# Offsets of matmul operands in SBUF: the low part of x's first quarter, one sum, and the first pair's kept weights

## The chip, the cores and the metric

The kernel runs on one core of a Trainium2 chip. The metric is the device time of one execution in microseconds; of the kernel before, three runs are at hand, and one further execution was profiled. Engines are named as in the profile: PE is TensorE (PEld its weight loads), DVE VectorE, ACT ScalarE, POOL GpSimd, SP SyncE.

## The reference

One decoder layer on x of 512 tokens by 1024 features, float32: a half-step SwiGLU FFN, a token mixer of two recurrent head groups, and a second half-step FFN, each between two RMS norms.

```python
x = x + 0.5 * rms_norm(swiglu_ffn(rms_norm(x, norm_pre[l, 0]), ffn1_w_in[l], ffn1_w_out[l]), norm_post[l, 0])
mixed = token_mixer(rms_norm(x, norm_pre[l, 1]), w_mix_in[l], ...)
x = x + rms_norm(mixed, norm_post[l, 1])
x = x + 0.5 * rms_norm(swiglu_ffn(rms_norm(x, norm_pre[l, 2]), ffn2_w_in[l], ffn2_w_out[l]), norm_post[l, 2])

def swiglu_ffn(x, w_in, w_out):
    gate, up = jnp.split(x @ w_in, 2, axis=-1)
    return (jax.nn.silu(gate) * up) @ w_out
```

The change touches the first product of the FFNs, x @ w_in, with 1024 rows and 2 x 2816 columns of weights.

## The kernel before

**Numbers in two parts.** A float32 value is held as a high part rounded to the matmul's format (fp32r) and a low part that is the rest. A product is three matmuls: high by high, high by low and low by high. ScalarE writes the high part of weights (L237), VectorE the low one (L239), out of a raw tile that a DMA filled.

**The FFN's first product.** The 22 column blocks of 128 are taken in 11 pairs (PAIRS). For a pair, x transposed is cut in four quarters by feature half and token half, the weights in four blocks a to d, and a scheme of seven products, p1 to p7, takes the place of the usual eight (products of sums of quarters). `prod` (L524) does one: 24 matmuls at L537, three parts by two column blocks of 128 by four k, each with 128x128 stationary weights and 128x256 moving values. The moving operand is `left[p]`: for p1 the quarter `xq[0]`, for p2 `xq[1]`; later p4 and p5 use `xq[3]` and `xq[2]`; p3, p6 and p7 use sums of quarters that lie in the three `s` tiles, `sq[0]`, `sq[2]`, `sq[1]`. For most products the parts come in the order high by high, high weights by the low moving part, low weights by the high moving part; c1 has the low moving part last.

Pair 0 is done by the usual eight products, because sums of quarters aren't there yet: c1 to c4 on the first token half (`xq[0]`, `xq[1]`), then e1 to e4 on the second with the same weights. Three of these weights (of c1, c3 and c4) are kept for e1, e3 and e4 in the `s` tiles, in the places `stay[1]`, `stay[2]`, `stay[0]`, before the sums overwrite them; c2's are in the ring of weights `w`. The order is written out by hand in `HEADS` and `ORDER` (L42 to L49): c1, c3, c2, c4, p1 of pair 1, e1, e3, e2, p1 of pair 2, p2 of pair 1, e4, p2 of pair 2, then p7, p5, p3, p6 of pair 1, p5, p7, p3, p4 (of pair 1), p6 of pair 2, then from pair 3 on p1, p4 of the pair before, p3, p5, p7, p6, p2 (in pair 3 a little different). In the first FFN `start` (L629) issues the head (c1 to p2 of pair 2), in the second `ffn_head` (L594). Transposes of x (L312) stand in the head: in the first FFN ahead of c4 and ahead of p1 of pair 1, in the second ahead of c3 and ahead of c4. In the first FFN one small transpose of parameters (L1020) stands ahead of p7 of pair 1.

**The second product** is at L794 and L802 in `ffn_out` (L765): there the weights move, and hidden values (`hs`, in the `s` tiles and in the tiles of x) are stationary. The mixer's projections read the same four tiles `xq` with the ordinary layout, through `xop` (L147).

**Places in SBUF.** `xq[n]` are four tiles of 2 x 1024 floats per partition (8192 bytes): high part, then low part, each four k of 256 tokens. The ring of weights is one tile `w` with room for four weights of 2 x 1024 floats, which `lie` (L202) places at PAD + 2048 n + d floats, with d of `LIES`. The `s` tiles have 2 x 1024 + PAD floats; sums lie in them from LATE = 112 floats on, except that the low part of the sum of p7 lies at 0 instead of at LATE + 1024: counted mod 512 bytes (128 floats) that is 64 bytes further. The kept weights lie at 0, except that the low part of the one of c1 lies at 1024 + NEAR (48 floats).

The head and the steady part of the first product are TensorE work in a fixed order; weights wait for a place in the ring (four in all, dropped after their product), and sums for the products that use what they overwrite.

The functions that the change touches, and those that call them:

Of the kernel before, what the change touches and what calls it, by code (L numbers as in the profile page):

```python
# [9 lines left out]
F32R = mybir.dt.float32r  # L10
# [4 lines left out]
P = 128  # L15
T = 512
D = 1024
# [2 lines left out]
ND = D // P  # L20
NF = FF // P
EPS = 1e-6
RAW, WBUF, PAD, LATE, NEAR, NEXT = 3, 4, 128, 112, 48, 64
PAIRS = NF // 2
HALF = T // 2
KH = ND // 2
# [40 lines left out]
class Load:  # L67


    def __init__(self, key, src, a, b, ring="raw", depth=3, ahead=3, group=None):  # L70
        self.key, self.src, self.a, self.b, self.ring, self.depth, self.ahead = key, src, a, b, ring, depth, ahead
        self.group = group
# [12 lines left out]
class Layer:  # L85
    def __init__(self, ctx, tc, aps):
        self.tc, self.nc = tc, tc.nc
        self.__dict__.update(aps)
        nc = self.nc
        pool = lambda name, **kw: ctx.enter_context(tc.tile_pool(name=name, bufs=1, **kw))  # L90
        self.cp, self.wp, self.sp, self.psp = pool("cp"), pool("wp"), pool("sp"), pool("psp", space=PSUM)
        self.uid, self.hold = 0, ()
        self.wt, self.free, self.slot = None, deque(), {}

        self.ident = self.cp.tile([P, P], F32, name="ident")
        make_identity(nc, self.ident)
        self.nhalf = self.cp.tile([P, 8], F32, name="nhalf")
        nc.gpsimd.memset(self.nhalf, -0.5)
        self.xs = self.cp.tile([P, NT, D], F32, name="xs")

        self.xq = [self.cp.tile([P, 2, KH, HALF], F32R, name=f"xq{n}") for n in range(4)]
        self.prm = self.cp.tile([P, 36], F32, name="prm")

    def nm(self, s):
# [42 lines left out]
    def xop(self, k, part, t0, t1):  # L147
        q = self.xq[2 * (t0 // HALF) + k // KH]
        return q[:, part, k % KH, t0 % HALF : (t1 - 1) % HALF + 1]
# [52 lines left out]
    def lie(self, kind):  # L202

        used = [o for _, o, _ in self.slot.values()]
        at = LIES[kind]

        first = 1 + (kind == "out")
        tries = [(n, d) for n in self.free for d in (at[:first] if n < 2 else at[first - 1 :: -1])]
        for n, d in tries + [(n, d) for d in at[first:] for n in self.free]:
            o = PAD + 2 * D * n + d  # L210
            if o + 2 * D <= self.wt.shape[1] and all(abs(o - a) >= 2 * D for a in used):
                return n, o

    def split(self):

        nc = self.nc
        it = self.items.popleft()
        raw = self.raw[it.key]
        _, a, b = raw.shape
        if it.dst:  # L220
            w = it.dst()
        else:
            if self.wt is None:
                self.wt = self.wp.tile([P, 2 * D * WBUF + 2 * PAD], F32R, name="w")
            if not self.slot and it.key[0] != "mix":
                self.free = deque(FREE)
            n, o = self.lie("out" if it.key[1] == "out" else "mix" if it.key[0] == "mix" and b == 512 else "any")
            self.free.remove(n)
            w = self.wt[:, o : o + 2 * D].rearrange("p (b k t) -> p b k t", b=2, k=a)
            self.slot[id(w)] = n, o, w  # L230
        hi, lo = self.both(w)
        if it.sums:
            raw, hi, lo = (self.flat(v)[:, QUARTER:] for v in (raw, hi, lo))
        self.ready.append((w, it.dst is not None))
        rows = it.rows
        if rows is None:
            nc.scalar.copy(hi, raw)  # L237
            yield
            nc.vector.tensor_tensor(lo, raw, hi.bitcast(F32), op=ALU.subtract)  # L239
        else:  # L240
            for j in range(a):
                nc.scalar.activation(hi[:, j], raw[:, j], AF.Copy, scale=rows[:, j : j + 1])
            yield
            for j in range(a):
                nc.vector.scalar_tensor_tensor(
                    lo[:, j], raw[:, j], rows[:, j : j + 1], hi[:, j].bitcast(F32), op0=ALU.mult, op1=ALU.subtract
                )
        with self.behind(*self.hold):
            for out, other in it.adds:
                o, c = self.raw[out], self.raw[other]  # L250

                late = out[1] >= HEAD
                (nc.vector if late else nc.gpsimd).tensor_tensor(o, o, c, op=ALU.add)  # L253
        if it.sums:
            self.sum_quarters(self.quarters(self.raw[it.key]))
        self.load_due(self.done)
        self.done += 1
        yield
# [14 lines left out]

        return w if isinstance(w, tuple) else (w[:, 0], w[:, 1])

    def place(self, t, a, late=False):

        o = LATE if late else 0
        return t[:, o : o + 2 * D].rearrange("p (b k t) -> p b k t", b=2, k=a)

    def feed(self, most=WBUF):

# [43 lines left out]
    def part(self, i, h, src):  # L326

        pv = self.turn(src, h)
        v = slice(i * P, (i + 1) * P)
        dst = self.xq[h][:, :, :, v]  # L330
        yield
        self.nc.scalar.copy(dst[:, 0], pv)
        yield
        self.nc.vector.tensor_tensor(dst[:, 1], pv, dst[:, 0].bitcast(F32), op=ALU.subtract)
        yield
        self.nc.scalar.copy(self.xf[h][:, :, v], pv)
        yield
# [167 lines left out]
    def open_ffn(self, ctx):  # L505

        hp = self.hpool = ctx.enter_context(self.tc.tile_pool(name=self.nm("hp"), bufs=1))
        self.hf = hp.tile([P, NF, T], F32, name=self.nm("hf"))
        self.xf = [self.hf[:, j : j + 2, :].rearrange("p a (b t) -> p (a b) t", t=HALF) for j in (NF - 4, NF - 2)]
        sq = [hp.tile([P, 2 * D + PAD], F32R, tag="s", bufs=3, name=self.nm("sq")) for _ in range(3)]  # L510
        self.sq = [self.place(t, KH, True) for t in sq]

        part = lambda o: sq[1][:, o : o + D].rearrange("p (k t) -> p k t", k=KH)
        self.sq = [self.both(self.sq[0]), (part(D + LATE), part(0)), self.both(self.sq[2])]
        xq = [self.both(x) for x in self.xq]
        self.stay = [self.place(t, KH) for t in sq]
        self.stay[1] = (self.stay[1][:, 0], sq[1][:, D + NEAR : 2 * D + NEAR].rearrange("p (k t) -> p k t", k=KH))
        self.left = {"p1": xq[0], "p2": xq[1], "p4": xq[3], "p5": xq[2], "p6": self.sq[2], "p7": self.sq[1], "p3": self.sq[0]}
        self.left.update({"c1": xq[0], "c2": xq[1], "c3": xq[0], "c4": xq[1]})
        self.left.update({"e1": xq[2], "e2": xq[3], "e3": xq[2], "e4": xq[3]})  # L520
        self.gs, self.held, self.copies = [], {}, []
        self.hs, self.bank, self.later, self.u, self.q, self.had = deque(), {}, deque(), {}, {}, set()
# [106 lines left out]
    def start(self, norm, xn):  # L629
# [8 lines left out]
        split = self.split()  # L638
        step(q[1][0], q[1][1])
        next(split)  # L640
        step(q[1][0])
        next(split)
        step(q[0][0], q[1][0])
        head = deque(HEADS)
# [74 lines left out]
    def x_place(self, *n):  # L719

        out = []
        for m in range(2):
            t = self.xq[n[m % len(n)]].rearrange("p b k t -> p (b k t)")
            o = PAD - LATE + NEXT + (D * m if len(n) == 1 else 0)
            out.append(t[:, o : min(o + D, 2 * D)])
        return out
# [949 lines left out]
```

## Time and profile before

| | us |
|---|---|
| three runs | 950.09, 950.67, 952.49 |
| median | 950.67 |
| profiled execution | 950.96 |
| its span, first to last instruction | 949.2 |
| PE busy | 938.8 |
| DVE busy | 774.5 |
| ACT busy | 489.4 |
| POOL busy | 119.4 |

The costliest groups of instructions on TensorE (busy us, mean ns of one, then idle time ahead of it):

```profile
L537 PE MATMUL ps<-xq,w 128*128 128x256 f32 x2016 | 237.9, 277 | 0.0
L537 PE MATMUL ps<-sq,w 128*128 128x256 f32 x1440 | 171.0, 277 | 0.0
L794 PE MATMUL ps<-w,hs 128*128 128x256 f32 x1344 | 158.9, 277 | 0.6 <-DVE ps L770 0.6
...
L482 PE MATMUL ps<-xq,w 128*128 128x256 f32 x480 | 56.4, 278 | 0.0
L802 PE MATMUL ps<-w,hs 128*128 128x256 f32 x336 | 40.3, 276 | 0.0
```

The page's group L537 `ps<-xq,sq` (288 matmuls in all) has the products of kept weights. Matmuls are pipelined: one is told with 276 ns or more from start to end, while the next starts some 113 to 118 ns later. So the pace is read from the differences between starts, not from the mean ns. In the order of time, matmuls of one line and the same tiles that follow each other without a gap stand as one row, with their count; the start of the next row less the start of this one is the time of the row. Offsets in a tile aren't in the profile; they come from the program.

### The profile page before, as it was taken

The page shows a single profiled execution, that of the slowest core. Times are in us where ns is not written, and L with a number is a line of the kernel's source. Part 1 is how long each engine was busy: PE and PEld are TensorE (multiplying, and loading weights), DVE is VectorE, ACT ScalarE, POOL GpSimd, SP SyncE. Part 2 cuts the span into 40 slices and gives each one's busy share as a digit, 9 for nine tenths or more (in the row PEclk, how much of TensorE's full clock was granted, in tenths as well). Part 3 has the DMA queues.
Part 4 walks back from the last instruction along what each step waited for, and adds up shares of the span by engine and source line. Part 5 has one row for each costly group of instructions (what it writes and reads, how often), then busy time and mean ns, then how long its engine had stood idle before and what let it go on. Part 6 is the DMA issues. An engine that isn't in the chain of part 4 may idle for free.

```text
span 949.2 us, 18146 instructions
## 1 busy us (share of the span) xinstructions
PE 938.8 (99%) x7531; PEld 905.0 (95%) x7531; DVE 774.5 (82%) x1052; ACT 489.4 (52%) x691; POOL 119.4 (13%) x176
## 2 busy tenths in 40 slices
PE   9999999999999999999999999999999999999997
PEld 7999999999999999998887888899999999999997
DVE  6899999999789776698846665797998899988983
ACT  7645444456446456956632444664444444654641
POOL 2530000000001045200011310354000000000101
PEclk9999999999999999999999999999999999999999
DMA  9244343344232024321212124324333333124202
GB/s 319 82 133 134 106 129 108 104 121 125 91 111 88 23 84 119 112 67 46 89 45 67 46 89 148 98 66 134 112 111 121 108 108 111 67 90 134 78 35 89
DMA packets 81677, 96.13 MB, mean 101 GB/s; under 512 B 4117, under 2 KB 61497, under 8 KB 81594
## 3 DMA queue, kind: packets, MB, share of 16 engines
q1 hardware_dynamic: 81306, 94.44, 31.4%
q8 instruction: 59, 0.97, 0.4%
q10 hardware_dynamic: 288, 0.52, 0.2%
q14 instruction: 24, 0.20, 0.1%
HBM read 92.85 MB, written 2.10 MB: 100 GB/s over the span
## 4 chain that ended last, share of the span: by engine, by line
PE 62%; DVE 1%; issue 0%; ACT 0%; POOL 0%; POOLq 0%; DVEq 0%; ACTq 0%
PE ps L537 23%; PE ps L794 8%; PE ps L482 6%; PE ps L143 5%; PE ps L145 5%; PE ps L144 5%; PE ps L802 3%; PE ps L1177 2%; PE ps L492 1%; PE ps L312 1%; PE ps L1351 0%; PE ps L1262 0%; PE ps L1458 0%; PE ps L1431 0%; PE ps L1217 0%; DVE w L239 0%
## 5 line engine op out<-in xcount | busy, mean ns | idle before, releaser
L237 ACT CAST w<-raw 128x1024 fp32r<-128x1024 f32 (+1 forms) x228 | 235.7, 1040 | 252.2 <-PE ps L537 92.0
L239 DVE TENSOR_TENSOR w<-raw,w 128x1024 fp32r<-128x1024 f32 (+1 forms) x228 | 281.8, 1242 | 42.0 <-ACT w L237 41.9
L537 PE MATMUL ps<-xq,w 128*128 128x256 f32 x2016 | 237.9, 277 | 0.0
L537 PEld LDWEIGHTS ps<-xq,w 128*128 128x128 f32 x2016 | 233.3, 188 | 0.0
L537 PE MATMUL ps<-sq,w 128*128 128x256 f32 x1440 | 171.0, 277 | 0.0
L537 PEld LDWEIGHTS ps<-sq,w 128*128 128x128 f32 x1440 | 167.4, 188 | 0.0
L794 PE MATMUL ps<-w,hs 128*128 128x256 f32 x1344 | 158.9, 277 | 0.6 <-DVE ps L770 0.6
L794 PEld LDWEIGHTS ps<-w,hs 128*128 128x128 f32 x1344 | 155.6, 188 | 0.9 <-issue 0.9
L253 DVE TENSOR_TENSOR raw<-raw,raw 128x1024 f32<-128x1024 f32 x64 | 80.1, 1252 | 0.6
L143 PE MATMUL ps<-w,xq 128*128 128x512 f32 x192 | 78.9, 411 | 0.1
L145 PE MATMUL ps<-w,xq 128*128 128x512 f32 x192 | 74.9, 392 | 0.0
L144 PE MATMUL ps<-w,xq 128*128 128x512 f32 x192 | 74.9, 391 | 0.0
L400 POOL TENSOR_SCALAR col<-col 128x1 f32<-128x1 f32 x24 | 10.1, 421 | 496.5 <-ACT junk L399 496.5
L482 PE MATMUL ps<-xq,w 128*128 128x256 f32 x480 | 56.4, 278 | 0.0
L482 PEld LDWEIGHTS ps<-xq,w 128*128 128x128 f32 x480 | 55.2, 188 | 0.5 <-issue 0.5
L253 POOL TENSOR_TENSOR raw<-raw,raw 128x1024 f32<-128x1024 f32 x16 | 43.1, 2695 | 51.2 <-DVE w L239 40.8
L143 PEld LDWEIGHTS ps<-w,xq 128*128 128x128 f32 x192 | 36.1, 188 | 8.3 <-issue 0.9
L145 PEld LDWEIGHTS ps<-w,xq 128*128 128x128 f32 x192 | 36.0, 188 | 8.1 <-DVE xq L319 0.3
L144 PEld LDWEIGHTS ps<-w,xq 128*128 128x128 f32 x192 | 36.2, 188 | 6.7 <-issue 0.2
L729 ACT CAST hs<-hf 128x1024 fp32r<-128x1024 f32 x28 | 29.4, 1050 | 22.2 <-PE ps L802 22.2
L802 PE MATMUL ps<-w,hs 128*128 128x256 f32 x336 | 40.3, 276 | 0.0
L802 PEld LDWEIGHTS ps<-w,hs 128*128 128x128 f32 x336 | 39.1, 188 | 0.0
(250 smaller groups left out, 1144.7 us busy)
## 6 DMA issues: line engine op xcount, KB each, us to landing
raw<-in_ffn_w_in_dram SPq DMA_DIRECT2D x88, 512.0 KB, 3.7
raw<-in_ffn_w_out_dram SPq DMA_DIRECT2D x44, 512.0 KB, 3.7
raw<-in_w_mix_in_dram SPq DMA_DIRECT2D x28, 512.0 KB, 3.7
raw<-in_w_mix_out_dram SPq DMA_DIRECT2D x8, 512.0 KB, 3.7
out_dram<-xs SPq DMA_DIRECT2D x8, 256.0 KB, 2.1
xs<-in_x_dram SPq DMA_DIRECT2D x6, 256.0 KB, 6.8
gpost<-in_norm_post_dram SPq DMA_DIRECT2D x3, 512.0 KB
gpre<-in_norm_pre_dram SPq DMA_DIRECT2D x2, 512.0 KB, 4.1
```

What stands on the lines that cost most here:

```text
L143: mm(ps, sh, mh, start=start, stop=False, **kw)
L144: mm(ps, sh, ml, start=False, stop=False, **kw)
L145: mm(ps, sl, mh, start=False, stop=stop, **kw)
L237: nc.scalar.copy(hi, raw)
L239: nc.vector.tensor_tensor(lo, raw, hi.bitcast(F32), op=ALU.subtract)
L253: (nc.vector if late else nc.gpsimd).tensor_tensor(o, o, c, op=ALU.add)
L482: mm(ps[:, u0:u1], w[:, a, k, :], self.xop(k, b, u0, u1), start=k + n + m == 0, stop=k == ND - 1 and n == 2, skip_group_check=True,)
L537: self.nc.tensor.matmul(ps[:, c], wb[b][:, k, v], left[d][:, k, :], start=first and a + n + k == 0, stop=n == 2 and k == KH - 1, skip_grou ...
L729: self.nc.scalar.copy(hi, src)
L794: mm(out, a[kk][:, i * P : (i + 1) * P], w[:, b, kk, QUARTER * v : QUARTER * (v + 1)], start=begin and c == kk == n == 0, stop=kk == 1 and ...
L802: mm(ps[:, QUARTER * c : QUARTER * (c + 1)], A[a][:, c], B[b], start=begin and c == n == 0, stop=n == 2, skip_group_check=True,)
L1177: nc.tensor.matmul(sc[:, 64 * m : 64 * m + 64], k8[:, m], q8[:, m], start=True, stop=True)
```

## The change

It moves operands; no instruction comes in or goes out.

- `xq[0]` becomes 2 x (1024 + 16) floats. In the view `xh[0]`, which `part` writes and which the products p1, c1 and c3 read, the low part lies 1024 + 16 floats behind the high one, so 64 bytes further mod 512 than before. The mixer and `x_place` keep the ordinary view of the same tile. The four tiles are allocated in the order 1, 2, 3, 0, the longer one last.
- The low part of the sum of p7 lies behind its high part like those of the other sums, at LATE + 1024.
- The kept weights lie at NEXT = 64 floats (256 bytes) in the `s` tiles, high and low part one behind the other, all three alike; NEAR is gone.
- The ring of weights begins at FRONT = 96 floats in its tile in place of PAD = 128, and the tile is 32 floats shorter; `xq[0]` is 32 floats longer.

```diff
-RAW, WBUF, PAD, LATE, NEAR, NEXT = 3, 4, 128, 112, 48, 64
+RAW, WBUF, PAD, LATE, NEXT, FRONT, STEP = 3, 4, 128, 112, 64, 96, 16
...
-        self.xq = [self.cp.tile([P, 2, KH, HALF], F32R, name=f"xq{n}") for n in range(4)]
+        xq = {n: self.cp.tile([P, 2 * D + 2 * STEP * (n == 0)], F32R, name=f"xq{n}") for n in (1, 2, 3, 0)}
+        self.xt = [xq[n] for n in range(4)]
+        self.xq = [t[:, : 2 * D].rearrange("p (b k t) -> p b k t", b=2, k=KH) for t in self.xt]
+
+        x0 = self.xt[0].rearrange("p (b x) -> p b x", b=2)[:, :, :D].rearrange("p b (k t) -> p b k t", k=KH)
+        self.xh = [x0, *self.xq[1:]]
...
-            o = PAD + 2 * D * n + d
+            o = FRONT + 2 * D * n + d
...
-                self.wt = self.wp.tile([P, 2 * D * WBUF + 2 * PAD], F32R, name="w")
+                self.wt = self.wp.tile([P, 2 * D * WBUF + FRONT + PAD], F32R, name="w")
...
-    def place(self, t, a, late=False):
-
-        o = LATE if late else 0
-        return t[:, o : o + 2 * D].rearrange("p (b k t) -> p b k t", b=2, k=a)
+    def place(self, t, o):
+
+        return t[:, o : o + 2 * D].rearrange("p (b k t) -> p b k t", b=2, k=KH)
...
-        dst = self.xq[h][:, :, :, v]
+        dst = self.xh[h][:, :, :, v]
...
-        self.sq = [self.place(t, KH, True) for t in sq]
-
-        part = lambda o: sq[1][:, o : o + D].rearrange("p (k t) -> p k t", k=KH)
-        self.sq = [self.both(self.sq[0]), (part(D + LATE), part(0)), self.both(self.sq[2])]
-        xq = [self.both(x) for x in self.xq]
-        self.stay = [self.place(t, KH) for t in sq]
-        self.stay[1] = (self.stay[1][:, 0], sq[1][:, D + NEAR : 2 * D + NEAR].rearrange("p (k t) -> p k t", k=KH))
+        self.sq = [self.both(self.place(t, LATE)) for t in sq]
+        xq = [self.both(x) for x in self.xh]
+        self.stay = [self.place(t, NEXT) for t in sq]
...
-            t = self.xq[n[m % len(n)]].rearrange("p b k t -> p (b k t)")
+            t = self.xt[n[m % len(n)]]
```

## The prediction

> **What bounds the kernel.** I read the page first, then the order of time of the matmuls, then the clock and the waits.
>
> ```profile
> PE 938.8 (99%) x7531; PEld 905.0 (95%) x7531; DVE 774.5 (82%) x1052; ACT 489.4 (52%) x691; POOL 119.4 (13%) x176
> ...
> PE ps L537 23%; PE ps L794 8%; PE ps L482 6%; PE ps L143 5%; PE ps L145 5%; PE ps L144 5%; PE ps L802 3%; PE ps L1177 2%; PE ps L492 1%; PE ps L312 1%; PE ps L1351 0%; PE ps L1262 0%; PE ps L1458 0%; PE ps L1431 0%; PE ps L1217 0%; DVE w L239 0%
> ```
>
> TensorE is busy 99% of 949.2 us and the chain of waits is made of its matmuls. No instruction is added or taken out, so only the pace of matmuls can change the time. That pace is read from the starts in the order of time (start us, us, then instruction and count); a row's 128x256 matmuls follow each other without a gap.
>
> ```profile
> 33.41 8.64 PE L537 MATMUL ps<-xq,w 128*128 128x256 f32 x72
> 41.90 2.99 PE L537 MATMUL ps<-xq,sq 128*128 128x256 f32 x24
> 44.72 2.99 PE L537 MATMUL ps<-xq,w 128*128 128x256 f32 x24
> 47.64 0.25 PE L1020 MATMUL ps<-ident,rows 36*128 36x36 f32 x1
> 47.82 3.10 PE L537 MATMUL ps<-sq,w 128*128 128x256 f32 x24
> 50.76 2.88 PE L537 MATMUL ps<-xq,w 128*128 128x256 f32 x24
> 53.48 5.60 PE L537 MATMUL ps<-sq,w 128*128 128x256 f32 x48
> 58.92 2.88 PE L537 MATMUL ps<-xq,w 128*128 128x256 f32 x24
> ```
>
> From 33.41 to 41.90, 72 matmuls take 8.49 us, 117.9 ns each. From 53.48 to 58.92, 48 of the same shape take 5.44 us, 113.3 ns each. So there are **two paces**: a product of 24 takes 2.83 us at the slow one and 2.72 us at the quick one, 0.11 us apart. The granted clock is 1.00 in both stretches (windows 24 to 47 and 53 to 81 us), so it is not the clock. The turn lies inside the product from 47.82 to 50.76: p7 of pair 1, the first product whose low moving part lies 64 bytes further. The second FFN does the same:
>
> ```profile
> 640.81 2.99 PE L537 MATMUL ps<-xq,sq 128*128 128x256 f32 x24
> 643.63 2.99 PE L537 MATMUL ps<-xq,w 128*128 128x256 f32 x24
> 646.46 3.00 PE L537 MATMUL ps<-sq,w 128*128 128x256 f32 x24
> 649.30 2.88 PE L537 MATMUL ps<-xq,w 128*128 128x256 f32 x24
> 652.02 5.60 PE L537 MATMUL ps<-sq,w 128*128 128x256 f32 x48
> ```
>
> 2.82 and 2.83 us, then p7 of pair 1 with 2.84, then 2.72. Two different products stand before it and one thing is common: the step of p7. I read it so: **the step of 64 bytes releases the slow pace**, for 0.01 us more than a slow product. In the quick pace the step has a price: p7 and its neighbour take 5.49 us, a pair without it 5.44 (53.48 to 58.92), so 0.05 us:
>
> ```profile
> 83.45 5.66 PE L537 MATMUL ps<-sq,w 128*128 128x256 f32 x48
> 88.94 8.32 PE L537 MATMUL ps<-xq,w 128*128 128x256 f32 x72
> ```
>
> **Places.** By the program's memory layout, counted mod 512 bytes, the quarters of x begin at 160, the places of weights in these products at 480, the three s tiles at 224. Nearly all stationary operands of the FFNs lie 320 bytes ahead of the moving one. Kept weights lie 64 ahead (224 - 160), the low part of the first pair's 256, p7's low part has its weights 256 ahead (480 - 224). After the change the kept weights lie at 320, p7 at 320, and p1, c1 and c3 meet their low moving part at 256: the geometry of p7, mod 512. The w tile begins 128 bytes later (xq0 is that much longer) and its places 128 earlier in it: they stay. Only small tiles behind xq and the raw ring move, by 128 bytes; VectorE and ScalarE read them, and no row shows a duration that hangs on this. Taken as nothing, covered by the lead that weights have over TensorE (below); slower reads would have to use up that lead before the end moved.
>
> **The sum, first FFN**, differences between starts, after minus before.
> - c1: enters slow, and exchanges its 8 matmuls with a step in the weights for 8 with a step in x. Between -0.11 (quick) and +0.01 (the second FFN's p7); the same kind of step in the same slow pace, so 0.
> - c3: quick after c1's step, with its own: 2.72 + 0.05 + 0.03 of c1's tail = 2.80 for 2.83, -0.03.
> - c2 -0.11. c4 follows transposes. Such an entry falls either way: rows after transposes begin slow at 338.89, 351.22 and 620.92, quick at 342.60 and 357.75. c4 was slow (2.91): 0, bounds -0.11 and 0.
> - p1 of pair 1, entered slow: +0.01 with the step (bounds -0.06, +0.01), and it releases.
> - e1 and e3, 5.67 (27.74 to 33.41) to 5.44: -0.23. e2, p1, p2: 8.49 to 8.21 (three quick, one step): -0.28. e4 2.82 to 2.72: -0.10. p2: -0.11. Together so far -0.85.
> - p7 of pair 1 follows the single small matmul at 47.64. Entered quick it loses 0.12. Entered slow it loses 0.01 and no step comes until p1 of pair 3: eight slow products are 0.85, p7 of pair 2 is in them without its step (-0.05), p1 enters slow and carries 0.07 more. Bounds of this place -0.12 and +0.90. The nearest rows are entries whose first start is late like this one: at 345.77 and 348.49 quick within a few matmuls, at 47.82 itself slow. I take quick, two of three.
> - Later, nine p7 lose and eight p1 gain the step: -0.05. First FFN -1.02.
>
> **Second FFN.** c1 0 (2.84 now). c3 was entered quick (2.81); with the step +0.05, entered slow some +0.11: +0.08. c2 quick already. c4 0. p1 +0.01. e1 and e3 -0.23, e2 to p2 -0.27, e4 -0.10, p2 -0.11, p7 -0.12, later -0.05. Sum -0.79.
>
> **Total -1.81 us**, from 949.2 to 947.4 of span and from 950.96 to 949.15 for the profiled execution. The median shown is 950.67, 0.29 below that execution; from it, **948.9**.
>
> **What could eat it.** 1.1 us are gained by 53 us, so weights must be ready as much earlier. VectorE ended p2's of pair 1 at 37.52 for a start at 39.07, p7's at 44.86 for 47.82, p3's at 51.41 for 53.48: slack 1.5 to 3.0 us against at most 1.1, so TensorE stays the bound; what is late next would be p3's weights.
>
> ```profile
> 36.30 1.22 DVE L239 TENSOR_TENSOR w<-raw,w 128x1024 fp32r<-128x1024 f32 x1 [0.74 <-ACT w L237]
> 42.25 2.61 DVE L239 TENSOR_TENSOR w<-raw,w 128x1024 fp32r<-128x1024 f32 x1 [0.36 <-ACT w L237]
> 50.20 1.21 DVE L239 TENSOR_TENSOR w<-raw,w 128x1024 fp32r<-128x1024 f32 x1
> ```
>
> **Rivals.**
> 1. Entries further on fall quick. The last stage, from 920.20 to some 942.7 us, is slow: 190 matmuls at 4.5 ns are 0.86 us. The same code at 321.66 turned quick after a few matmuls, so an execution can have it either way (39 matmuls each):
>
> ```profile
> 321.66 4.70 PE L794 MATMUL ps<-w,hs 128*128 128x256 f32 x39 [0.30 <-DVE ps L770]
> 920.20 4.83 PE L794 MATMUL ps<-w,hs 128*128 128x256 f32 x39 [0.30 <-DVE ps L770]
> ```
>
>    With c4 and p1 quick in both FFNs and the short slow stretches after 338.89, 351.22, 394.91 and 416.4 (some 120 matmuls, 0.53 us) up to 1.75: **948.0, down to 947.2**.
> 2. p7 of pair 1 is entered slow: 1.02 given back, **949.9**.
> 3. Entries that were quick fall slow: after 357.75, some 310 matmuls (1.4 us), after 321.66 some 137 (0.6). **950.3 to 950.9**. Any shift in time can throw these, for and against.
> 4. The other side: the step releases only in p7, because something beyond the place mod 512 counts (there the low part lies below the high one in its tile). It decides as soon as c1 and p1 leave the pace slow. Then 2 x 65 products after p7 keep 0.106 us each, 13.8; the L794 and L802 stages up to their first wait some 820 matmuls in each FFN at 4.5 ns, 7.4; less the 20 steps of p7, 1.0: about +20, **971**. Against: both FFNs show one release, mod 512 alike.
> 5. Places count for nothing and the release at p7 has another cause at the same point. Then the heads stay slow and the time is **950.7**. For: c3 at 614.60 ran quick at distance 64, so a distance does not set the pace by itself. Against: the turn in the same product twice, and 5.49 against 5.44 wherever p7 stands later.
>
> The Trainium skill, page "TensorE: Matmul & The Clock Gate", section "Part 2: What happens when you issue a matmul", says that the next tile's weight load, on a read port of its own, takes no SBUF read bandwidth from the running matmul. By that rule the operands' places are free and the change is worth nothing, rival 5's time; the 117.9 and 113.3 ns of one shape at one clock speak against it, without showing where the 4.5 ns go.
>
> **Chances.** Forecast 0.32, rival 1 0.28, rival 2 0.21, rival 3 0.07, rival 4 0.06, rival 5 0.06. The bound for a difference is 0.3%, 2.85 us, about what a measurement of this kernel can tell from no change. Faster than 947.8: most of rival 1 (0.22) and the lower edge of the forecast (0.05), 0.27. Slower than 953.5: rival 4 and the edge of rival 3, 0.08. Within: 0.65. Range: from rival 1's low end to the lesser of rival 3's prices with rival 2's 1.02 on top (950.3 + 1.0): 947.2 to 951.3; outside lie rival 4 and the far corner of rival 3.
>
> **What will show it.** Right: products from c2 to p2 of pair 2 start 2.72 us apart, p7 and p6 later 5.44 apart, p1 and its neighbour 5.49, the rows after 53 us as before but 1 us earlier. Wrong: 2.83 after c3 or p1; 2.83 between p7 and p1 of pair 3 would be rival 2; TensorE with idle ahead of an L537 product would mean that weights bound the head.

## The result, and the profile after

| | before | after |
|---|---|---|
| median of 19 runs each, us | 950.70 | 948.91 |
| lowest and highest | 950.04, 954.43 | 947.97, 950.61 |
| profiled execution, its span | 950.96, 949.2 | 950.09, 948.4 |

The ratio is 0.9977, 95% interval 0.9969 to 0.9985: a gain of 0.15 to 0.31%. The interval leaves out 1, but the gain is at most about the 0.3% that a difference had to reach to count as one. Forecast was 948.9, within 947.2 to 951.3.

The page of the kernel after (busy us and instructions of PE, then groups: busy us, mean ns of one, idle). TensorE still bounds everything and has lost 1.0 us of busy time at the same count of matmuls:

```profile
PE 937.8 (99%) x7531; PEld 903.4 (95%) x7531; DVE 775.8 (82%) x1052; ACT 489.2 (52%) x691; POOL 119.6 (13%) x176
...
L537 PE MATMUL ps<-xq,w 128*128 128x256 f32 x2016 | 237.8, 277 | 0.0
...
L537 PE MATMUL ps<-sq,w 128*128 128x256 f32 x1440 | 169.8, 276 | 0.0
```

The matmuls of the kernel after in the order of time, first FFN (start us, us from first start to last end, instruction, count):

```profile
27.73 5.60 PE L537 MATMUL ps<-xq,sq 128*128 128x256 f32 x48
33.17 8.38 PE L537 MATMUL ps<-xq,w 128*128 128x256 f32 x72
41.38 2.88 PE L537 MATMUL ps<-xq,sq 128*128 128x256 f32 x24
...
82.63 5.60 PE L537 MATMUL ps<-sq,w 128*128 128x256 f32 x48
88.07 8.38 PE L537 MATMUL ps<-xq,w 128*128 128x256 f32 x72
```

e1 and e3 take 27.73 to 33.17, 5.44 us, where 5.67 stood; e2, p1 and p2 take 8.21 where 8.49 stood, 0.05 of it p1's step; p7 and p6 from 82.63 take 5.44, the step having left them. In the kernel before, p1 of pair 1 and then e1 with e3 were:

```profile
24.83 3.07 PE L537 MATMUL ps<-xq,w 128*128 128x256 f32 x24
27.74 5.83 PE L537 MATMUL ps<-xq,sq 128*128 128x256 f32 x48
```

Second FFN of the kernel after, same view:

```profile
621.74 3.07 PE L537 MATMUL ps<-xq,sq 128*128 128x256 f32 x24
624.65 3.00 PE L537 MATMUL ps<-xq,w 128*128 128x256 f32 x24
627.49 5.60 PE L537 MATMUL ps<-xq,sq 128*128 128x256 f32 x48
632.93 8.38 PE L537 MATMUL ps<-xq,w 128*128 128x256 f32 x72
```

c4 (621.74 to 624.65) is slow, p1 takes 2.84, and e1 starts a run of 2.72 that lasts (2.77 where p1 steps): the slow pace ends in the first product with the step, as p7 had ended it before.

Since both kernels issue the same 7531 matmuls in the same order, the starts of the same matmul can be subtracted. The table shows the time from one matmul to another in the profiled executions of both (the second product is counted from its first matmul; the last p4 of the first product lies behind that):

| stretch | before | after | difference |
|---|---|---|---|
| start to c1 | 11.73 | 11.97 | +0.24 |
| c1, c3, c2 of the first FFN | 8.61 | 8.39 | -0.22 |
| transposes and c4 to the small transpose ahead of p7 of pair 1 | 27.30 | 26.55 | -0.75 |
| from there to its second product | 177.68 | 177.53 | -0.15 |
| its second product | 112.78 | 112.78 | 0 |
| passage from the first FFN into the mixer | 22.47 | 24.07 | +1.60 |
| mixer, to c1 of the second FFN | 250.39 | 250.44 | +0.05 |
| c1, c3, c2 of the second FFN | 9.17 | 9.22 | +0.05 |
| transposes and c4 to its second product | 203.73 | 202.86 | -0.87 |
| its second product | 118.91 | 118.10 | -0.81 |

The +1.60 is a matter of the clock, not of the pace. Matmuls of the kernel after between 344 and 352 us, then the windows there (window, us, busy us and count per engine, PEclk, the granted clock, DMA share, GB/s):

```profile
344.90 1.19 PE L496 MATMUL ps<-xq,w 128*128 128x256 f32 x8 [0.21 <-ACT w L242]
347.62 3.66 PE L496 MATMUL ps<-xq,w 128*128 128x256 f32 x16 [1.52 <-DVE w L244]
351.08 1.10 PE L316 MATMUL ps<-ident,xn 128*128 128x128 f32 x8
```

```profile
344.38:347.79 3.41, 1.68 (x12) 1.28 (x12) 3.41 (x6) 2.74 (x5) 0.51 (x1) 1.00 0.00 0
346.00:348.00 2.00, 0.47 (x3) 0.38 (x3) 2.00 (x3) 1.12 (x3) 0.71 (x1) 0.95 0.00 0
348.00:349.00 1.00, 1.00 (x7) 1.00 (x6) 1.00 (x2) 0.00 (x0) 0.92 (x2) 0.50 0.21 35
...
351.00:352.00 1.00, 1.00 (x11) 1.00 (x9) 0.97 (x1) 0.92 (x3) 0.91 (x1) 0.90 1.03 295
```

After a wait of 1.52 us for weights the clock was granted at one half for some 3.4 us, and 16 matmuls took 3.46 us (347.62 to 351.08). The kernel before has the same wait of 1.52 us and the full clock after it:

```profile
348.49 2.10 PE L492 MATMUL ps<-xq,w 128*128 128x256 f32 x16 [1.52 <-DVE w L239]
350.43 1.03 PE L312 MATMUL ps<-ident,xn 128*128 128x128 f32 x8
```

There the same 16 take 1.94 us. The difference lies in a grid of time. In the traces' record of the granted clock, every change in all 14 profiles comes a whole number of steps of 3.413 us after the clock was first full: in the kernel after, the clock was first full at 9.87 us, the drop at 347.79 is 99 steps behind that, the return at 351.20 is 100. In the step that ends at 347.79 (the first window above) TensorE was idle for 3.41 less 1.68, 1.73 us: the wait of 1.52 and the one of 0.21 ahead of 344.90. The second profile of this kernel has 1.75 there and the half clock too. In the kernel before the wait of 1.52 ends in the next step, and this one has 1.51:

```profile
344.88:348.29 3.41, 1.90 (x15) 1.50 (x13) 3.41 (x6) 3.10 (x5) 0.14 (x1) 1.00 0.00 0
```

None of the other twelve profiles has more than 1.53 in any step between the first full clock and the end of its matmuls. So the half clock goes with how the waits fall on the grid; that the places of operands have another part in it than by shifting the waits is not shown.

And the last stage, which was slow, fell quick (39 matmuls, 920.15 to 924.68, 4.53 us; before, 4.67 to the same point):

```profile
920.15 4.69 PE L794 MATMUL ps<-w,hs 128*128 128x256 f32 x39 [0.30 <-DVE ps L770]
924.68 0.84 PE L794 MATMUL ps<-w,xq 128*128 128x256 f32 x6
```

### The profile page after: what moved, and what is told of

Read it like the earlier page. It is cut to its first block, busy times and chain, and to the rows that moved or that the text cites. A ratio compares the mean times of both kernels' runs of the same rounds, so it can differ in the third digit from the quotient of the medians.

```text
span 948.4 us, 18148 instructions
## 1 busy us (share of the span) xinstructions
PE 937.8 (99%) x7531; PEld 903.4 (95%) x7531; DVE 775.8 (82%) x1052; ACT 489.2 (52%) x691; POOL 119.6 (13%) x176
## 4 chain that ended last, share of the span: by engine, by line
PE 62%; DVE 1%; issue 0%; ACT 0%; POOL 0%; POOLq 0%; DVEq 0%; ACTq 0%
PE ps L537 22%; PE ps L794 8%; PE ps L486 6%; PE ps L148 5%; PE ps L150 5%; PE ps L149 5%; PE ps L802 3%; PE ps L1177 2%; PE ps L496 1%; PE ps L316 1%; PE ps L1351 0%; PE ps L1262 0%; PE ps L1458 0%; PE ps L1431 0%; PE ps L1217 0%; DVE w L244 0%
```

## The experiments

Distances are the place of the stationary operand less that of the moving one, mod 512 bytes, from the programs' memory layout. The normal one is 320, the step of the changed kernel makes 256. The first seven kernels below were timed 4 to 12 times beside the kernel before on the same chip (median 951.5 there), and one execution of each was profiled; the rest are single executions. Below, a product's time is from its first start to that of the next product.

**No step at all.** The changed kernel with the ordinary view of x's first quarter everywhere.

```diff
-        self.xh = [x0, *self.xq[1:]]
+        self.xh = self.xq
```

> The kernel after with no step anywhere: c1, c3 and p1 read x's first quarter in the ordinary layout, kept weights stay at 320. Theory (the step releases the slow pace): a product that is entered slow, c4 of the second FFN above all, hands the slow pace on until the next break in TensorE's stream: 2.83 us a product from c4 on, through p7 of pair 1 and to the end of the first product, and 117.8 ns in the L794 and L802 stages. One FFN so is about +11 us, both +21, less the 24 steps of 0.053 (1.3): 957 to 970. Rival (the kept weights' place brought the gain and the step nothing): 948.9 less 1.3 = 947.6, all heads quick.

958.92 us, ratio to before 1.0077 (1.0064 to 1.0091). The first FFN was quick without any step: c1 entered quick, c4 was slow, p1 of pair 1 entered quick again after the transposes, and so it stayed. In the second FFN (order of time; the rows are p1, e1 with e3, and e2 with p1 and p2) nothing ended the slow pace of c4:

```profile
622.65 2.99 PE L537 MATMUL ps<-xq,w 128*128 128x256 f32 x24
625.48 5.82 PE L537 MATMUL ps<-xq,sq 128*128 128x256 f32 x48
631.13 8.64 PE L537 MATMUL ps<-xq,w 128*128 128x256 f32 x72
```

2.83 us a product from 622.65 to the end. From the transposes ahead of c4 on the first product took 210.04 us against 202.86, the second product 122.37 against 118.10. So the step is what ends the slow pace in the second FFN, and the slow pace is handed on to the second product; in the first FFN another cause was at work.

**The kept weights alone.** The kernel before with them where all others lie; the step stays in p7.

```diff
-        self.stay = [self.place(t, KH) for t in sq]
-        self.stay[1] = (self.stay[1][:, 0], sq[1][:, D + NEAR : 2 * D + NEAR].rearrange("p (k t) -> p k t", k=KH))
+        self.stay = [t[:, NEXT : NEXT + 2 * D].rearrange("p (b k t) -> p b k t", b=2, k=KH) for t in sq]
```

> The kernel before with its step in p7 as it was, and only the kept weights moved to 320 ahead. Theory: the heads stay as they are entered, slow products of 2.83 us from c4 to p2 of pair 2 in the second FFN, release at p7 of pair 1: 950.0 to 950.7. Rival (place of the kept weights): heads at 2.72 us a product, 948.9 or less.

950.45 us, ratio 0.9992 (0.9983 to 1.0001). First FFN: quick from c1 (c4 apart), 26.45 us from the transposes ahead of c4 to the small transpose where before had 27.30. Second FFN: slow from c4 to p7 of pair 1, which took 2.84 and released, as before. The rows are e1 with e3, first FFN, then second:

```profile
28.22 5.60 PE L536 MATMUL ps<-xq,sq 128*128 128x256 f32 x48
...
628.06 5.82 PE L536 MATMUL ps<-xq,sq 128*128 128x256 f32 x48
```

So the theory held in the second FFN and the rival in the first: with the kept weights moved the first head was quick without a step in x, and the second was not helped.

**The step in x alone.** The changed kernel with the kept weights at their old places (distance 64; the low part of c1's weight, also read by e1, at 256).

```diff
-        self.stay = [self.place(t, NEXT) for t in sq]
+        self.stay = [self.place(t, 0) for t in sq]
+        self.stay[1] = (self.stay[1][:, 0], sq[1][:, D + 48 : 2 * D + 48].rearrange("p (k t) -> p k t", k=KH))
```

> The kernel after with the step in x's first quarter, but the kept weights where they were in the kernel before (64 ahead, the low part of c1's 256). Theory: the step in c1, c3 and p1 releases at these distances too; products of 2.72 us from p1 of pair 1 on, 948.9 to 949.4. Rival (place): heads slow to p1 of pair 1 or further, c3 and e1 at 2.83, 950.5 to 951.

949.88 us, ratio 0.9982 (0.9973 to 0.9990), between the two expectations. First FFN in the order of time:

```profile
28.98 5.76 PE L538 MATMUL ps<-xq,sq 128*128 128x256 f32 x48
34.58 8.55 PE L538 MATMUL ps<-xq,w 128*128 128x256 f32 x72
42.96 2.88 PE L538 MATMUL ps<-xq,sq 128*128 128x256 f32 x24
```

p1 ahead of these rows was quick, but e1 and e3 take 5.60 us: inside e1 the starts are 113 ns apart up to the low weights, 120 in them and 118 from then on. A step of the stationary operand **threw the quick pace into the slow one**; p1 of pair 2, in the row from 34.58 (8.38), released it. The second FFN did the same: p1 released, e1 threw it back, p1 of pair 2 released. In c1 of the first FFN the same happens: 113 ns ahead of its low weights, 120 in them. So in the second FFN a quick head needs both parts of the change; in the first the place of the kept weights was enough (the kernel above).

**p7's step kept as well.** The changed kernel with p7's low part still 64 bytes further.

```diff
+        part = lambda o: sq[1][:, o : o + D].rearrange("p (k t) -> p k t", k=KH)
+        self.sq[1] = (part(D + LATE), part(0))
```

> The kernel after with the step in p7 as well. Theory: 20 more steps of 0.053 us in the quick pace, +1.06: 950.0, p7 at 2.77 us each. Rival (p7 of pair 1 was often entered slow in the kernel after, and lost about 1 us then): its step would get that back in those executions, so less than +0.6 in the median, 949.5 or less.

949.94 us, ratio 0.9984 (0.9975 to 0.9993), against 948.91 of the changed kernel. From the small transpose ahead of p7 of pair 1 to the second product 178.06 us in the first FFN against 177.53, from the transposes ahead of c4 203.39 against 202.86 in the second: 0.53 each for ten products, so **a step costs 0.053 us** in the quick pace.

**Fewer steps.** x's first quarter is ordinary; the step lies in the third quarter as e1 and e3 read it, two in each FFN.

```diff
...
-        self.xh = [x0, *self.xq[1:]]
+        self.xh, self.xe = self.xq, x2
...
-        self.left.update({"e1": xq[2], "e2": xq[3], "e3": xq[2], "e4": xq[3]})
+        xe = self.both(self.xe)
+        self.left.update({"e1": xe, "e2": xq[3], "e3": xe, "e4": xq[3]})
```

(x2 is the third quarter's view with the step; its tile is the longer one.)

> The step of 64 bytes is taken out of x's first quarter and put into x's third quarter as e1 and e3 read it: two steps in each FFN in place of twelve. Theory (a step of the moving operand releases the slow pace and costs 0.053 us in the quick one): twenty steps fewer, 20 x 0.053 = 1.06 us less; in the second FFN c4 and p1 of pair 1 stay slow (2.83 each, p1 was 2.84 with its step) and e1 releases, so e3 and all later products take 2.72 and p1 of later pairs 2.72 in place of 2.77. 947.9 us, ratio to the changed kernel 0.9989. Rival (the release needs the step often, since products fall slow again later): some products after 60 us or after 665 us at 2.83, and the time at or above the changed kernel's 948.9. Rival (the release needs x's first quarter): the second FFN stays slow as in e1_no_step, about 958.5.

948.54 us, ratio 0.9963 (0.9950 to 0.9977). Second FFN in the order of time:

```profile
624.90 5.77 PE L538 MATMUL ps<-xq,sq 128*128 128x256 f32 x48
630.51 8.32 PE L538 MATMUL ps<-xq,w 128*128 128x256 f32 x72
638.67 2.88 PE L538 MATMUL ps<-xq,sq 128*128 128x256 f32 x24
```

p1 ahead of these rows was slow, e1 releases (2.84 of the 5.61), then 8.16 for three products without a step; all products behind the head of each FFN take 2.72 (66 each; p7 of pair 1, entered behind the small transpose of the first FFN, 2.84). Against the changed kernel the first FFN's first product is 0.54 us shorter (c1 to c2 0.11, the rest 0.43: ten steps fewer at 0.053), the second's 0.39, because there p1 stays slow and it is e1 that carries the release. Together 0.93 where 1.06 was forecast. In whole executions the two can't be told apart: their ratios' intervals overlap.

**The changed kernel again,** unedited.

> The changed kernel as it is, beside e8_step_in_e on the same chip: 948.9 us, within 0.6. What it tells besides: which entries repeat from one profiled execution to the next. If the pace at an entry is set by the instructions alone, c1 of the first FFN is quick again, c4 slow in both, p1 of pair 1 quick in the first and slow in the second, the last stage quick. If it is set by chance, some of these differ.

948.87 us, ratio 0.9973 (0.9962 to 0.9984). Every entry was as in the first profile: c1 quick, c4 slow in both FFNs, p1 of pair 1 quick in the first and slow in the second, the last stage quick, and the half clock was there again (24.09 us in that passage). For one program on the same data the pace at these entries repeated in two of two profiles.

**A step of the stationary operand.** No step in x; the low part of each kept weight 64 bytes lower.

```diff
-        self.xh = [x0, *self.xq[1:]]
+        self.xh = self.xq
...
-        self.stay = [self.place(t, NEXT) for t in sq]
+        part = lambda t, o: t[:, o : o + D].rearrange("p (k t) -> p k t", k=KH)
+        self.stay = [(part(t, D + NEXT), part(t, NEXT - STEP)) for t in sq]
```

> No step in x and none in p7; the low part of each kept weight lies 64 bytes lower, so that the kept products meet their low part at a distance of 256 bytes mod 512 by a step of the stationary operand. Theory (only a step of the moving operand releases, a step of the stationary one can throw a quick product into the slow pace): the second FFN stays slow from c4 to its end as in e1_no_step, and products e1, e2, e3, e4 with kept weights throw the first FFN slow as well, with no release: between 958.5 and 966. Rival (the distance of 256 counts, whichever operand makes it): the kept products release, e1 takes about 2.77 to 2.84, all after it 2.72: about 948.

970.84 us, ratio 1.0200 (1.0181 to 1.0219). First FFN:

```profile
28.75 5.77 PE L538 MATMUL ps<-xq,sq 128*128 128x256 f32 x48
34.37 8.64 PE L538 MATMUL ps<-xq,w 128*128 128x256 f32 x72
```

p1, ahead of these rows, was quick, e1's low weights turned it slow, and the row from 34.37 takes 8.47 for three products. Both FFNs then stayed at 2.83 to their ends. The direction was as expected, the price above the 966 given: the expectation left out the second products, which took 116.30 and 121.62 us against 112.78 and 118.10. So 256 bytes of distance is not what releases; it counts which operand steps.

**A step of 128 bytes,** in p7 alone.

```diff
-        self.xh = [x0, *self.xq[1:]]
+        self.xh = self.xq
...
+        self.sq[1] = (part(D + LATE), part(0 + 16))
```

> No step in x; p7's low part lies 128 bytes further in place of the 64 it has in the kernel before: distance 192 mod 512. Theory (a step of the moving operand releases, its size not being what counts as long as it is under 512): p7 of pair 1 of the second FFN releases, everything after it takes 2.72 and p7 2.77: head slow as before, about 949.8. Rival (256 bytes, half of 512, is the place that releases): no release, the second FFN slow to its end, about 958.9.

969.41 us: the theory in this form fell, and the rival's 958.9 was missed too, because the first FFN turned slow. First FFN:

```profile
47.15 3.08 PE L539 MATMUL ps<-sq,w 128*128 128x256 f32 x24
50.06 2.99 PE L539 MATMUL ps<-xq,w 128*128 128x256 f32 x24
52.88 5.82 PE L539 MATMUL ps<-sq,w 128*128 128x256 f32 x48
```

p7 entered quick (47.15; within eight matmuls its starts were 113 ns apart) and left slow; p5 behind it takes 2.82. In the second FFN the slow pace passed through p7 unchanged. A step of 128 bytes does the opposite of one of 64.

**Steps of 32 bytes, and of 64 bytes the other way,** in p7 alone, x's first quarter ordinary as above.

```diff
...
+        self.sq[1] = (part(LATE), part(D + LATE + 8))
```

```diff
...
+        self.sq[1] = (part(D + LATE), part(LATE - 16))
```

> No step in x; p7's low part lies 32 bytes further in place of the 64 it has in the kernel before: distance 288 mod 512. Reading so far (a step of 64 bytes releases the slow pace; one of 128 bytes does not, and turns a quick product slow): open for 32. If what counts is a small step that does not reach as far as 128, it releases: p7 of pair 1 in the second FFN is the last slow product, the first FFN stays quick, about 949.8. If 64 bytes is the only size that releases, 32 does nothing: the second FFN slow to its end, about 958.9 with a quick first FFN, 969.4 if it turns quick into slow as 128 did. Taken as likelier: it releases.

> No step in x; p7's low part lies 64 bytes lower in place of 64 higher: distance 384 mod 512. If the size of the step alone counts, it releases: about 949.8. If the direction counts (the low part must be met at a shorter distance to its weights than 320), no release: 958.9 with a quick first FFN, 969.4 if it turns quick into slow. Taken as likelier: no release.

951.60 and 951.05 us, one execution each (949.89 for the kernel before beside them). Both release. The one of 32 bytes in the second FFN:

```profile
647.80 2.99 PE L539 MATMUL ps<-sq,w 128*128 128x256 f32 x24
650.63 2.88 PE L539 MATMUL ps<-xq,w 128*128 128x256 f32 x24
653.35 5.60 PE L539 MATMUL ps<-sq,w 128*128 128x256 f32 x48
```

p7 takes 2.83, then 2.72. For the step back no release was held likelier, and that was wrong: p7 took 2.85 and everything after it 2.72. In the quick pace the two cost 0.067 and 0.080 us. Their whole times hold other things: with 32 bytes a wait of 0.5 us ahead of p2 of pair 2 and a slow stretch in the mixer (1.6 us, rival 3's entry), with -64 a slow last stage (0.8).

**Distances held throughout.** No step; the ring of weights and the kept weights 64 bytes lower (shown), or higher (NEXT = 80, FRONT = 112).

```diff
-RAW, WBUF, PAD, LATE, NEXT, FRONT, STEP = 3, 4, 128, 112, 64, 96, 16
+RAW, WBUF, PAD, LATE, NEXT, FRONT, STEP = 3, 4, 128, 112, 48, 80, 16
...
-        self.xh = [x0, *self.xq[1:]]
+        self.xh = self.xq
```

> No step anywhere, but all weights of the FFNs' first product lie 64 bytes lower, kept ones too, so that every matmul there works at a distance of 256 bytes mod 512. It tells whether 256 is a quick place by itself or only one that is passed through. If quick by itself: products take 2.72 everywhere, the slow pace is not found at all, and the time is 947.5 to 949. If only passed through (the eight matmuls of a step take 113 to 125 ns, 118 on average): products of 2.83 or more throughout, 156 products by 0.106 us more, about 965 to 970. Taken as likelier: passed through only, near 969.

> As e11_all_256 with all weights of the FFNs' first product 64 bytes higher: a distance of 384 bytes mod 512 throughout, no step. If two paces exist at 320 alone, this has one pace, quick (947.5 to 949) or slow (965 to 970). If they exist at every distance, it goes as e1_no_step: first FFN quick, second slow from c4 on, about 958.9. Taken as likelier: as e1_no_step.

978.36 and 973.93 us. The edits did not give one distance throughout, as expected of them: the s tiles moved with the length of the ring. Lower, x stands at 256 to the ring and 192 to the kept weights, and the sums stay at 320; higher, 384, 448 and 320. The lower one in the first FFN:

```profile
34.44 8.80 PE L537 MATMUL ps<-xq,w 128*128 128x256 f32 x72
43.08 2.88 PE L537 MATMUL ps<-xq,sq 128*128 128x256 f32 x24
```

Held at 256, 72 matmuls take 8.64 us, 120.0 ns each, slower than the slow pace; e4 behind them, at 192, takes 2.72. Held at 384 the same products took 2.845 to 2.853, 118.7 ns. Neither distance is quick by itself, and the slow pace was seen at 192 and 448 too. 256 is passed through, as held likelier there, though at a higher price than the 970 given; that 384 would be like 320 was wrong.

## Why the prediction was right

- **Two paces, apart from the clock.** Held. Apart from the first few matmuls behind an entry, products at 320 without a step took 2.72 or 2.83 us in every profile, other than in the two with distances held throughout, where some behind a product at another distance took 2.73 to 2.75.
- **The step releases.** Held in the second FFN: c1 2.84 (taken unchanged), c1 to c2 +0.05 for +0.08, c4 unchanged, p1 2.84 (+0.01), then e1 to the end of the first product. The terms from c4 on sum to -0.87, and -0.87 was measured. Without the step the same FFN stayed slow.
- **First FFN, the sum.** -0.85 to p2 of pair 2; from c4 on -0.75 was measured for -0.71, c1 to c2 -0.22 for -0.14, and c1 began 0.24 later. Over all profiles c1 began between 11.48 and 13.16 us, and the starts of kernels that are alike up to there lie as far apart (11.48 with p7's step of 32 bytes, 12.25 with that of 128), so that is taken as no effect of this change. e1 and e3 gave 0.23, e2 to p2 0.28, as worked out. p7 of pair 1 was entered quick, as taken (rival 2 did not come), the later steps gave -0.05. Sum -0.88 for -1.02; without c1's later start it is -1.12.
- **First FFN, the reason.** Here a step of the prediction failed: "p1 of pair 1, entered slow: +0.01 with the step ... and it releases". p1 was entered quick, as c1 was, and without any step in it (no step at all, the kept weights alone) this head was as quick. At the old places a quick entry is of no use: the low weights of e1 turn it slow (the step in x alone). c1's low weights did so too. The prediction gave the kept weights' place no price of its own, and it is what lets a quick entry last through this head. p1's step released nothing here, as there was nothing to release; the sum came out because both readings end with e1 to p2 at the quick pace, so for this head the number is luck. Why c1 and p1 entered slow in the profile of the kernel before stays open: the kernel with the step in x alone has its kept weights at the same places, and both entered quick.
- **Price of the step.** 0.053 us measured for 0.05.
- **What could eat it.** In the kernel after TensorE never waited for weights ahead of these products, and the second product of the first FFN took 112.78 us in both.
- **Rival 1** came as well: the last stage fell quick in both profiles of the changed kernel, -0.81 for -0.86 worked out. Among the six experiments with other kernels whose second FFN was quick by then it fell quick in three and slow in three, so it is not shown to belong to the change. **A term that no part held** stood against it: the half clock, +1.60. The profiled pair sums to -0.86 by the table, and the executions differ by 0.87.
- **The medians, partly luck.** What the change aimed at measured -1.12 and -0.82 in the two FFNs, -1.94 for the -1.81 forecast, and the medians differ by 1.79. The half clock is hardly in them: of the 19 runs of the kernel after two have a mean granted clock of 0.996 (the profiled one and one of 950.61 us), the others 0.998 or 0.999; the two profiles with the half clock have 0.996 and 0.997, the other twelve 0.998 or more. How often the last stage or another entry fell quick in runs without a profile, nothing shows; so that the medians meet the forecast so closely is partly luck.
- **Rival 3's** entry after 357.75 stayed quick in both profiles of the changed kernel. It does fall slow at times: with the kept weights alone, and with p7's step of 32 bytes, the mixer took 1.6 us more.
- **Rival 5** (places count for nothing) fell with the kernel without a step, whose second FFN went slow through p7 of pair 1 and on to its end.
- **Rival 4** (releases only in p7) fell with the first profile. Its price was right: with both FFNs slow to their ends the 128-byte step measured 969.4, the weights' step 970.8, for some 971.
- **The Trainium skill's rule**, page "TensorE: Matmul & The Clock Gate", section "Part 2: What happens when you issue a matmul", that the next weight load takes no SBUF bandwidth from a running matmul, can't be the whole of it: 113.3 and 117.8 ns at the same places, and 120.0 at others, were measured for one shape at a granted clock of 1.00.

What the matmuls do in these two paces is not settled. A moving operand that steps by 32, 64 or -64 bytes for eight matmuls releases, one that steps by 128 turns the quick pace slow, and so does a stationary operand that steps by -64 or by 192. No rule of the distance alone fits these. Other sizes, and a step of other length than eight matmuls, were not tried.

## What to carry to other kernels

Where back-to-back matmuls of one shape show two pitches at one granted clock, read the starts, not the mean, and look at the places of both operands mod 512 bytes: 4% of the stage can hang on it, and it is handed on from product to product until something ends it. What paid here: keep stationary operands at one place, let one moving operand per stage step by 64 bytes soon after each entry that may be slow, and no more often, since each step costs 0.053 us. Subtract starts of the same matmul in two traces before believing a sum: here two effects of 0.8 and 1.6 us that the change did not aim at stood beside its own.

## What the runs showed of the hardware

- Pace is a state: 113.3 or 117.8 ns a matmul at the same places. Without a step the slow one was kept over 73 products in a row and into the next stage (second FFN, 2.83 us each; second product 122.37 us for 118.10).
- The entry behind eight transposes goes the same way again and again: c4 was slow in both FFNs in every profile with its weights at 320, p1 of pair 1 quick in the first FFN in all of these, c3 quick in the second. Of the kernels whose p1 starts at 320 there, the kernel before alone had it slow.
- The granted clock fell to 0.50 for 3.41 us in two of 14 profiles, both of the changed kernel, where TensorE had been idle for 1.73 and 1.75 us of one step of a grid of 3.413 us. The other twelve had at most 1.53 in any step, kept the full clock, and took 22.1 to 22.6 us for the passage from the first FFN into the mixer. Where between 1.53 and 1.73 the turn lies, no run shows. The Trainium skill, page "TensorE: Matmul & The Clock Gate", section "Part 1: The HAM clock gate (the "warmup" mystery)", tells of a half clock after an idle window of some 3.4 us, on windows that run freely. The half clock, its length and the grid agree; that a whole window must be idle does not, for half of one was enough here.
